# A ReGLU MLP with Strassen-Winograd products: w2 in two column halves, its sums accumulated earlier, the casts of later x moved, and GpSimd's loads held behind the first x rows

## The chip, the cores and the metric

The kernel runs on one core of a Trainium2 chip. The metric is the device time of one execution in microseconds; the times given are the median of three runs. A profile is one further execution taken by the hardware profiler; its span goes from the first to the last instruction.

## The reference

```python
def reference(x, w1, w2):              # x [16, 256, 512], w1 [512, 4096], w2 [2048, 512], all float32
    h = x @ w1
    gate, value = np.split(h, 2, axis=-1)
    h = np.maximum(gate, 0) * value
    return (h @ w2).astype(np.float32)
```

That is 4096 rows of x; a first product to 4096 hidden columns (2048 gates, 2048 values), a product of the two, and a second product back to 512 columns.

## The kernel before

All of it is in `fast_way` (`general_way` runs only if a flag computed from the data says that the numbers don't fit float16; here it doesn't). The 4096 rows are four sets (`NS`) of 1024, each in two halves of 512 (`TH`). Weights and x are float16 on the chip.

**First product.** The 2048 gate columns and as many value columns make 16 blocks (`NJ`) of 128 + 128. A block computes a 2 x 2 product (halves of the 512 inner rows, gate and value, halves of the set) with seven products instead of eight: `P1` to `P7`, each two matmuls of 512 columns. For that it needs sums of x (`S1` to `S4`, `x_sum`, on VectorE) and sums of w1 (`T1` to `T4`, `w1_ops`, L157): for blocks 4 to 15 GpSimd makes them in set 0, for blocks 0 to 3 VectorE does, later. Blocks 0 to 3 of set 0 are therefore computed plainly (`Plain`, L236), with eight products. `PERIOD` and `SLOT` (L25) interleave the seven products of neighbouring blocks.

**Second product.** `mm2_stream` (L271) multiplies the float16 result g by w2 in the same way: seven products P1 to P7 over 8 x 128 rows, for four groups of 128 rows of x, with sums `S1` to `S4` of g (`g_sum`, L264) and sums `T1` to `T4` of w2 (tiles `v_t`). The sums of g are made by GpSimd (S3, and most of S1) and by VectorE (the rest) in set 0. The stream is a Python generator of single matmuls: a set's first 20 are put between its last blocks, its last 8 between the first blocks of the next set, and the rest between the two (`advance`, L337).

**Loads.** x rows of set 0's first half come in float32 by SP (`xf`, in the tile of g's S1; L389), and are turned by TensorE (`turn_pair`, L361: transposes into PSUM, then copies). The first two blocks of w1 come in float32 by ACT (`wl`) and are cast by ACT and VectorE (`cast_w`). Everything else is cast to float16 by DMAs that GpSimd issues: the second half of set 0's x and, later, sets 1 to 3 into DRAM tiles `x16` (`cast_x`, L349), from where SP's transposing DMAs bring them in turned (`turn_by_dma`, L369) and plain row loads bring them for the data check (`fetch_rows`, L379, read by `look_x`); w1 in five more chunks (`fetch_w1`, L342); w2 in four parts of 512 KB, each 4 x 128 full rows (`fetch_w2`, L346). `w2_sb` holds w2 as [128, 16, 512], so the quarters B11, B12, B21, B22 (`V`, L148) have rows of 256 columns = 512 bytes within rows of 1024 bytes.

**The sums of w2** are made by DMA: SP copies a quarter into a `v_t` tile, and GpSimd issues a DMA that adds another quarter to it (`accum_op=ADD`): T1 = B11 + B12, T3 = B12 + B22, T2 = T1 + B22, T4 = T2 + B21 (L506 to L513, L522).

**What sets the order.** The schedule is manual: each engine runs its instructions, the issues of its DMAs among them, in the order in which the program text emits them; semaphores for data are put in by the framework. The order on GpSimd in set 0 is: the identity; the cast of x's second half; ten loads of w1; w1 sums of blocks 4, 5; two loads of w2; sums of blocks 6, 7; two loads of w2; sums of blocks 8, 9; three casts of x; sums of blocks 10, 11; the additions for T1 and T3; sums of blocks 12 to 15; the addition for T2; two S3 sums of g; the addition for T4; two S3 sums; three S1 sums. In sets 1 to 3 it has only sums of g.

Of the kernel before, what the change touches and what calls it, by code (L numbers as in the profile page):

```python
# [9 lines left out]
F32, F32R, F16 = dt.float32, dt.float32r, dt.float16  # L10
# [6 lines left out]
P = 128  # L17
TH = 512
# [81 lines left out]
def fast_way(ctx, tc, x2, w1, w2, out2, flag):  # L100
# [27 lines left out]
    place = {jb + i: (c, i) for c, (jb, n) in enumerate(CHUNKS) for i in range(n)}  # L128
    wr = [wpool.tile([P, 4, 2, n * P], F16, name=f"wr{c}") for c, (_, n) in enumerate(CHUNKS)]
    wt = [wpool.tile([P, 4, 2, n * P], F16, name=f"wt{c}") for c, (_, n) in enumerate(CHUNKS)]  # L130
    w2_sb = wpool.tile([P, NJ, DO], F16, name="w2_sb")
    v_t = {n: wpool.tile([P, NHC, HALF], F16, name=f"v_{n}") for n in ("T1", "T2", "T3", "T4")}
    x16 = {s: dpool.tile([SET, D], F16, name=f"x16_{s}") for s in range(NS)}

    NX = 2 * 2 * NB * NS
    NW = NX + 2 * NP
# [2 lines left out]
    def W(name, jb, n=1):  # L139
        c, i = place[jb]  # L140
        raw = {"B11": (0, 0), "B21": (2, 0), "B12": (0, 1), "B22": (2, 1)}
        js = slice(i * P, (i + n) * P)
        if name in raw:
            e, g = raw[name]
            return wr[c][:, e:e + 2, g, js]
        return wt[c][:, int(name[1]) - 1, :, js]

    V = {"B11": w2_sb[:, :NHC, :HALF], "B12": w2_sb[:, :NHC, HALF:], "B21": w2_sb[:, NHC:, :HALF], "B22": w2_sb[:, NHC:, HALF:],  # L148
         **{n: t for n, t in v_t.items()}}

    TURNS = (("T1", "B12", "B11", ADD), ("T2", "B22", "T1", ADD), ("T3", "B22", "B12", ADD), ("T4", "B21", "T2", ADD))

    def turned(op):
        for t in TURNS:
            op(*t)

    def w1_ops(eng, jb, n):  # L157
        turned(lambda m, a, b, o: eng.tensor_tensor(W(m, jb, n), W(a, jb, n), W(b, jb, n), op=o))  # L158

    warm = tmp.tile([P, 2, TH], F32, name="warm", tag="tmp")  # L160
    warm_b = warm.rearrange("p a t -> p (a t)").bitcast(F16)
    nc.vector.memset(warm[:, 0], 0.0)
    ident = wpool.tile([P, P], F32, name="ident")

    def idle(n):
        for _ in range(n):
# [14 lines left out]
    def look(t, at, of):  # L181
        sq = tmp.tile([P, 1024], F16, name="sq", tag="sq", bufs=1)
        sq = sq[:, :of] if len(t.shape) == 2 else sq[:, :of].rearrange("p (a b) -> p a b", a=t.shape[1])
        nc.scalar.activation(sq, t, SQUARE, scale=(P / of) ** 0.5, accum_out=st[:, at:at + 1])  # L184
# [159 lines left out]
        nc.gpsimd.dma_start(out=wr[c][:, :, g], in_=w1_v[:, :, g, jb * P:(jb + n) * P])  # L344

    def fetch_w2(i):  # L346
        nc.gpsimd.dma_start(out=w2_sb[:, 4 * i:4 * i + 4, :], in_=w2_v[:, 4 * i:4 * i + 4, :])  # L347

    def cast_x(s):  # L349
        nc.gpsimd.dma_start(out=x16[s], in_=x2[s * SET:(s + 1) * SET, :])  # L350
# [5 lines left out]

    g, go = g_tiles()
    xf = go["S1"].rearrange("p a t -> p (a t)").bitcast(F32).rearrange("p (b d) -> p b d", b=NB)
    wl = g[:, NJ - 4:].rearrange("p a t -> p (a t)").bitcast(F32).rearrange("p (e g j) -> p e g j", e=4, g=2)

    def turn_pair(o, b0):  # L361
        for b in (b0, b0 + 1):
            ps = psw.tile([P, 4, P], F32, name="W", tag="W")
            for e in range(4):
                nc.tensor.transpose(ps[:, e], xf[:, b, e * P:(e + 1) * P], ident)
            copy = nc.scalar.copy if b % 2 else nc.vector.tensor_copy
            copy(out=o["A1"][:, :, b * P:(b + 1) * P], in_=ps)

    def turn_by_dma(s, o, h):  # L369
        for k in range(2):  # L370
            nc.sync.dma_start_transpose(out=o[f"A{h + 1}{k + 1}"], in_=x16[s][h * TH:(h + 1) * TH, k * 256:k * 256 + 256])
# [7 lines left out]
    def fetch_rows(s, q):  # L379
        rows[s, q] = xpool.tile([P, 2, D], F16, name=f"xn{q % 2}")  # L380
        nc.sync.dma_start(out=rows[s, q], in_=x16[s][q * 256:(q + 1) * 256].rearrange("(b p) d -> p b d", p=P))

    def look_x(s, i):
        b = i // 2
        t = rows[s, b // 2][:, b % 2] if (s, b // 2) in rows else xf[:, b]
        look(t[:, i % 2 * 256:i % 2 * 256 + 256], 4 * NB * s + i, 256)

    for b in (0, 2):
        nc.sync.dma_start(out=xf[:, b:b + 2], in_=x_v[0, :, b:b + 2])  # L389
    for g_ in range(2):  # L390
        nc.scalar.dma_start(out=wl[:, :, g_], in_=w1_v[:, :, g_, :2 * P])
    make_identity(nc, ident)
    nc.gpsimd.dma_start(out=x16[0][TH:], in_=x2[TH:SET, :])
    for c in range(1, len(CHUNKS)):
        for g_ in range(2):
            fetch_w1(c, g_)

    xo = x_tiles()
    turn_by_dma(0, xo, 1)
    for q in (2, 3):  # L400
        fetch_rows(0, q)
    plain = [Plain(g, jb) for jb in range(NPLAIN)]
    idle(NWARM)
    cast_w(0)
# [15 lines left out]
    for p in plain[2:]:  # L420
        p.open_x()
        p.open_w()
        p.mm(0, xo["A1"], 0, 2)
        p.mm(1, xo["A1"], 0, 2)
        p.close(0)
    sums = list(SUMS)

    def x_sum(o):
# [3 lines left out]
    for p in plain:  # L432
        p.open_x()
        p.open_w()
        p.mm(0, xo["A2"], 0, 2)
        p.mm(1, xo["A2"], 0, 2)
        x_sum(xo)
        if p is not plain[-1]:
            p.close(1)
        look_x(0, p.jb)  # L440
# [3 lines left out]
        look(wr[c][:, :, i % 2, o * P:(o + 2) * P], NX + i, 1024)  # L444

    def look_w2(i):
        look(w2_sb[:, 2 * i:2 * i + 2].rearrange("p h n -> p (h n)"), NW + i, 1024)

    def judge():
        n = st.shape[1]  # L450
# [26 lines left out]
            BESIDE[s, 7 + 2 * i] = [f]  # L477
    BESIDE[NS - 1, 6] = [judge]
    verdict = []
    BESIDE[NS - 1, 20] = [lambda: tc.mark_branch_hint_location("general")]  # L480
    BESIDE[NS - 1, 18] = [lambda: verdict.append(nc.values_load(
        flag[0:1, 0:1], min_val=0, max_val=1, skip_runtime_bounds_check_because="a comparison wrote it"))]

# [3 lines left out]
    for s in range(NS):  # L487
        if s:
            g, go = g_tiles()
        first = NPLAIN if s == 0 else 0  # L490
        blocks = {jb: Block(xo, g, jb) for jb in range(first, NJ)}
        plan = {jb * PERIOD + at: (jb, n) for jb in blocks for n, at in SLOT.items()}
        last = NJ * PERIOD
        stream = mm2_stream(s, go)
        if s == 0:
            w1_ops(nc.gpsimd, 4, 2)
            fetch_w2(0)
            fetch_w2(1)
            w1_ops(nc.gpsimd, 6, 2)
            fetch_w2(2)  # L500
            fetch_w2(3)
            w1_ops(nc.gpsimd, 8, 2)
            for c in range(1, NS):
                cast_x(c)
            w1_ops(nc.gpsimd, 10, 2)
            nc.sync.dma_start(out=V["T1"], in_=V["B11"])  # L506
            nc.sync.dma_start(out=V["T3"], in_=V["B12"])
            nc.gpsimd.dma_start(out=V["T1"], in_=V["B12"], accum_op=ADD)  # L508
            nc.gpsimd.dma_start(out=V["T3"], in_=V["B22"], accum_op=ADD)  # L509
            nc.sync.dma_start(out=V["T2"], in_=V["T1"])  # L510
            w1_ops(nc.gpsimd, 12, 4)
            nc.gpsimd.dma_start(out=V["T2"], in_=V["B22"], accum_op=ADD)
            nc.sync.dma_start(out=V["T4"], in_=V["T2"])  # L513
        for at in range(first * PERIOD, last + PERIOD):
            if at in plan:
                jb, n = plan[at]
                if n == "P1" and s and jb in (4, 8):
                    fetch_rows(s, 1 + jb // 4)
                if n == "P1" and s == 0 and jb in (11, 12, 13, 14):
                    g_sum(nc.gpsimd, go, "S3", 2 * jb - 22, 2 * jb - 20)  # L520
                    if jb == 12:
                        nc.gpsimd.dma_start(out=V["T4"], in_=V["B21"], accum_op=ADD)  # L522
                getattr(blocks[jb], n)()
                if n == "P5":
                    for f in LOOKS.get((s, jb), ()):
                        f()
                if n == "P4" and s:
                    if jb < NHC:
                        g_sum(nc.gpsimd, go, "S3", jb, jb + 1)
                    elif jb < NJ - BY_DVE:  # L530
                        for m in ("S1", "S2", "S4"):
                            g_sum(nc.gpsimd, go, m, jb - NHC, jb - NHC + 1)
            elif at >= last:
                advance(stream, 4)
            else:
                advance(prev, 4)
        if s == 0:
            for h in (0, 2, 4):
                g_sum(nc.gpsimd, go, "S1", h, h + 2)
            g_sum(nc.vector, go, "S1", 6, 8)  # L540
            for m in ("S2", "S4"):
                for h in (0, NHC // 2):
                    g_sum(nc.vector, go, m, h, h + NHC // 2)
        else:
            for m in ("S1", "S2", "S4"):
                g_sum(nc.vector, go, m, NHC - BY_DVE, NHC)
        done = 20
        if s + 1 < NS:
            xo = x_tiles()
            for h in range(2):  # L550
                turn_by_dma(s + 1, xo, h)
            for q in range(2):
                fetch_rows(s + 1, q)
            advance(stream, 100)
            sums = list(SUMS)
            for _ in SUMS:
                x_sum(xo)
            if s == 0:
                w1_ops(nc.vector, 0, 2)
                w1_ops(nc.vector, 2, 2)  # L560
            advance(stream, MM2 - TAIL - 100 - done)
        else:
            advance(stream, MM2)
        prev = stream
# [29 lines left out]
```

## Time and profile before

| what | us |
|---|---|
| median of three runs (lowest, highest) | 345.38 (344.56, 346.49) |
| the profiled execution, its own time | 344.94 |
| its span | 343.2 |
| TensorE (PE) busy | 308.5, 90% of the span |
| VectorE (DVE), ScalarE (ACT), GpSimd (POOL) busy | 217.8, 188.1, 152.6 |
| mean granted TensorE clock | 0.960 |

The profile names an instruction by its line, engine, operation and tiles (written <- read). A number in brackets behind it is the time that its engine was idle before it, and what released it. Matmuls are pipelined, so that the shown length of the last of a group overlaps with the next group; starts are the better measure. SPq or POOLq is the issue of a DMA by SP or GpSimd; its landing is told apart from it. Where a window is named, times count from the span's start. Three of the page's rows by 40 equal slices of the span (8.6 us each; tenths of busy time, or of the full TensorE clock) show where the engines rest:

```
PE   6589993099469999999999999999999999999993
POOL 7289900685940013469900043399500144699000
PEclk9789999579969999999999999999999999999999
```

### The profile page before, as it was taken

The page shows a single profiled execution, that of the slowest core. Times are in us where ns is not written, and L with a number is a line of the kernel's source. Part 1 is how long each engine was busy: PE and PEld are TensorE (multiplying, and loading weights), DVE is VectorE, ACT ScalarE, POOL GpSimd, SP SyncE. Part 2 cuts the span into 40 slices and gives each one's busy share as a digit, 9 for nine tenths or more (in the row PEclk, how much of TensorE's full clock was granted, in tenths as well). Part 3 has the DMA queues.
Part 4 walks back from the last instruction along what each step waited for, and adds up shares of the span by engine and source line. Part 5 has one row for each costly group of instructions (what it writes and reads, how often), then busy time and mean ns, then how long its engine had stood idle before and what let it go on. Part 6 is the DMA issues. An engine that isn't in the chain of part 4 may idle for free.

```text
span 343.2 us, 5085 instructions
## 1 busy us (share of the span) xinstructions
PE 308.5 (90%) x1843; PEld 182.0 (53%) x1843; DVE 217.8 (63%) x328; ACT 188.1 (55%) x449; POOL 152.6 (44%) x133
## 2 busy tenths in 40 slices
PE   6589993099469999999999999999999999999993
PEld 3344441035348744444688544444887444446883
DVE  1147884048997278888843488888551788888401
ACT  2137673045138576667477576666585766764230
POOL 7289900685940013469900043399500144699000
PEclk9789999579969999999999999999999999999999
DMA  7999999788943200100551300100732001000113
GB/s 225 219 204 215 206 240 209 125 135 147 152 71 122 94 31 32 32 0 0 89 158 70 116 32 0 31 2 21 162 128 94 31 31 32 0 1 2 61 63 129
DMA packets 39069, 31.83 MB, mean 93 GB/s; under 512 B 16016, under 2 KB 34192, under 8 KB 38928
## 3 DMA queue, kind: packets, MB, share of 16 engines
q0 software_dynamic: 11728, 11.54, 21.4%
q1 hardware_dynamic: 26112, 18.75, 19.9%
q10 hardware_dynamic: 1200, 1.18, 1.1%
q8 instruction: 16, 0.26, 0.3%
q14 instruction: 13, 0.11, 0.1%
HBM read 24.64 MB, written 12.06 MB: 107 GB/s over the span
## 4 chain that ended last, share of the span: by engine, by line
PE 75%; DMA 15%; POOL 7%; issue 1%; DVE 0%; ACT 0%; POOLq 0%; SPq 0%
PE Y L196 20%; PE W L196 13%; PE X L196 13%; PE Y L278 12%; PE W L278 9%; PE X L278 7%; DMA v_T<-w_sb 6%; DMA w_sb<-in_w_dram 5%; DMA wr<-in_w_dram 4%; POOL g_S L267 3%; POOL wt L158 2%; POOL wr L344 1%; POOL v_T L509 1%; POOL v_T L508 0%; POOL w_sb L347 0%
## 5 line engine op out<-in xcount | busy, mean ns | idle before, releaser
L267 POOL TENSOR_TENSOR g_S<-g 128x512 f16<-128x512 f16 (+1 forms) x49 | 64.4, 1382 | 126.8 <-DVE g L233 124.8
L196 PEld LDWEIGHTS <-wt 128*128 128x128 f16 x480 | 47.0, 98 | 71.3 <-POOL wt L158 14.7
L196 PE MATMUL Y<-x_S,wt 128*128 128x512 f16 x240 | 72.3, 383 | 0.0
L196 PE MATMUL X<-x_A,wr 128*128 128x512 f16 x240 | 71.8, 381 | 0.2 <-ACT Y L203 0.2
L223 DVE SCALAR_TENSOR_TENSOR cc<-W,pu 128x512 f32<-128x512 f32 x60 | 41.5, 692 | 36.9 <-ACT pu L217 35.0
L278 PEld LDWEIGHTS <-g_S 128*128 128x128 f16 x512 | 50.2, 99 | 15.8 <-POOL g_S L267 8.9
L196 PEld LDWEIGHTS <-wr 128*128 128x128 f16 x360 | 35.3, 98 | 42.0 <-issue 2.1
L203 ACT COPY Y<-X 128x512 f32<-128x512 f32 x60 | 34.2, 570 | 39.3 <-PE X L196 20.5
L229 DVE SCALAR_TENSOR_TENSOR cc<-Y,pu 128x512 f32<-128x512 f32 x60 | 40.9, 682 | 14.5 <-PE Y L196 14.4
L196 PE MATMUL W<-x_S,wt 128*128 128x512 f16 x120 | 36.1, 383 | 13.8 <-POOL wt L158 13.8
L217 ACT ACTIVATE pu<-Y 128x512 f32<-128x512 f32 x60 | 35.9, 598 | 15.3 <-PE Y L196 15.3
L210 ACT ACTIVATE pu<-W 128x512 f32<-128x512 f32 x60 | 36.1, 602 | 14.5 <-PE W L196 14.3
L224 DVE SCALAR_TENSOR_TENSOR g<-X,cc 128x512 f16<-128x512 f32 x60 | 41.5, 692 | 2.3
L233 DVE SCALAR_TENSOR_TENSOR g<-Y,cc 128x512 f16<-128x512 f32 x60 | 40.9, 681 | 2.7 <-PE Y L196 2.7
L278 PEld LDWEIGHTS <-g 128*128 128x128 f16 x384 | 37.6, 98 | 8.2
L196 PE MATMUL W<-x_S,wr 128*128 128x512 f16 x120 | 36.2, 383 | 0.0
L196 PE MATMUL Y<-x_A,wt 128*128 128x512 f16 x120 | 35.9, 380 | 0.0
L278 PE MATMUL X<-w_sb,g 128*128 128x256 f16 x256 | 31.2, 272 | 0.0
L278 PE MATMUL Y<-v_T,g_S 128*128 128x256 f16 x256 | 30.7, 273 | 0.0
L308 DVE SCALAR_TENSOR_TENSOR o<-W,pv 128x256 f32<-128x256 f32 x16 | 6.8, 425 | 33.9 <-PE W L278 33.4
L278 PE MATMUL W<-v_T,g_S 128*128 128x256 f16 x128 | 17.9, 288 | 7.8 <-POOL g_S L267 7.8
L184 ACT ACTIVATE sq<-xn 128x256 f16<-128x256 f16 x56 | 23.2, 415 | 0.0
(64 smaller groups left out, 303.3 us busy)
## 6 DMA issues: line engine op xcount, KB each, us to landing
out_dram<-o SPq DMA_DIRECT2D x16, 256.0 KB, 2.1
out_dram<-pv SPq DMA_DIRECT2D x15, 256.0 KB, 2.0
xn<-x SPq DMA_DIRECT2D x14, 256.0 KB, 3.2
x<-in_x_dram POOLq DMA_DIRECT2D x3, 1024.0 KB, 18.7
wr<-in_w_dram POOLq DMA_DIRECT2D x4, 512.0 KB, 20.3
w_sb<-in_w_dram POOLq DMA_DIRECT2D x4, 512.0 KB, 14.8
v_T<-w_sb POOLq DMA_DIRECT2D x4, 512.0 KB, 8.3
wr<-in_w_dram POOLq DMA_DIRECT2D x6, 256.0 KB, 13.4
```

Of the source, the lines that this page charges most:

```text
L158: turned(lambda m, a, b, o: eng.tensor_tensor(W(m, jb, n), W(a, jb, n), W(b, jb, n), op=o))
L184: nc.scalar.activation(sq, t, SQUARE, scale=(P / of) ** 0.5, accum_out=st[:, at:at + 1])
L196: nc.tensor.matmul(ps, W(wn, self.jb)[:, b], self.xo[xn][:, b, :], start=fresh and b == 0, stop=b == 1, skip_group_check=True)
L203: nc.scalar.copy(out=self.Y, in_=self.X)
L210: nc.scalar.activation(self.p5, self.W, COPY, scale=GS)
L217: nc.scalar.activation(self.u2, self.Y, COPY, scale=-GS)
L223: nc.vector.scalar_tensor_tensor(out=self.c12, in0=self.W, scalar=GS, in1=self.u2, op0=MULT, op1=ADD)
L224: nc.vector.scalar_tensor_tensor(out=self.g[:, self.jb, :TH], in0=self.X, scalar=0.0, in1=self.c12, op0=MAX, op1=MULT)
L229: nc.vector.scalar_tensor_tensor(out=self.c22, in0=self.Y, scalar=-GS, in1=self.p5, op0=MULT, op1=ADD)
L233: nc.vector.scalar_tensor_tensor(out=self.g[:, self.jb, TH:], in0=self.Y, scalar=0.0, in1=self.c22, op0=MAX, op1=MULT)
L267: eng.tensor_tensor(go[n][:, h0:h1], go[i0][:, h0:h1], go[i1][:, h0:h1], op=op)
L278: nc.tensor.matmul(ps, go[gn][:, k, b * P:(b + 1) * P], V[vn][:, k, :], start=fresh and k == 0, stop=k == NHC - 1, skip_group_check=True)
```

## The change

- w2 lies in two tiles `w2_h`, one for each half of its columns, as [128, 16, 256], so that a quarter is one stretch of 4 KB in each partition. It is loaded as four quarters of 512 KB (8 x 128 rows of 256 columns).
- SP copies B11, B12, B22, B21 into T1, T3, T2, T4, one after the other; no copy waits for an addition any more. GpSimd's additions are T1 += B12, T3 += B22, T2 += T1, T4 += T2. The first two are issued after two of the four w1 sums of blocks 12 to 15, the third after all four, the last in block 12 as before.
- Set 0's second half of x doesn't go through DRAM: GpSimd's DMA casts it into `xh` (the tile of g's S2), and TensorE turns it with a float16 identity (`turn_half`). `turn_by_dma` and `fetch_rows` of set 0 go.
- GpSimd's first load waits until the first x rows have landed (a copy of one column into `gate`), and x's second half comes after w1's chunk 1 instead of ahead of it.
- The casts of sets 1 to 3 move: set 1's behind the fourth S3 sum in set 0, those of sets 2 and 3 to the first products of blocks 0 and 1 of set 1.
- The hint for the branch at the end names five engines.

```diff
-    w2_sb = wpool.tile([P, NJ, DO], F16, name="w2_sb")
+    w2_h = [wpool.tile([P, NJ, HALF], F16, name=f"w2_{i}") for i in range(2)]
...
-    x16 = {s: dpool.tile([SET, D], F16, name=f"x16_{s}") for s in range(NS)}
+    x16 = {s: dpool.tile([SET, D], F16, name=f"x16_{s}") for s in range(1, NS)}
...
+    V = {f"B{k + 1}{n + 1}": w2_h[n][:, k * NHC:(k + 1) * NHC] for k in range(2) for n in range(2)}
+    V.update(v_t)
...
+    def w1_ops(eng, jb, n):
         for t in TURNS:
-            op(*t)
-
-    def w1_ops(eng, jb, n):
-        turned(lambda m, a, b, o: eng.tensor_tensor(W(m, jb, n), W(a, jb, n), W(b, jb, n), op=o))
+            w1_one(eng, jb, n, *t)
+
+    def w1_one(eng, jb, n, m, a, b, o):
+        eng.tensor_tensor(W(m, jb, n), W(a, jb, n), W(b, jb, n), op=o)
+
+    def add_w2(m, v):
+        nc.gpsimd.dma_start(out=V[m], in_=V[v], accum_op=ADD)
...
-    ident = wpool.tile([P, P], F32, name="ident")
+    ident = {t: wpool.tile([P, P], t, name=f"ident{k}") for k, t in enumerate((F32, F16))}
+    gate = wpool.tile([P, 1], F32, name="gate")
...
     def fetch_w2(i):
-        nc.gpsimd.dma_start(out=w2_sb[:, 4 * i:4 * i + 4, :], in_=w2_v[:, 4 * i:4 * i + 4, :])
+        ks, n = slice(i // 2 * NHC, i // 2 * NHC + NHC), i % 2
+        nc.gpsimd.dma_start(out=w2_h[n][:, ks], in_=w2_v[:, ks, n * HALF:(n + 1) * HALF])
...
+    xh = go["S2"][:, :NB]
...
+    def turn_half(o, b0, copy):
+        ps = psx.tile([P, 4, 2, P], F16, name="X", tag="X")
+        for b in range(2):
+            for e in range(4):
+                nc.tensor.transpose(ps[:, e, b], xh[:, b0 + b, e * P:(e + 1) * P], ident[F16])
+        copy(out=o["A2"][:, :, b0 * P:(b0 + 2) * P], in_=ps.rearrange("p e b t -> p e (b t)"))
...
-        t = rows[s, b // 2][:, b % 2] if (s, b // 2) in rows else xf[:, b]
+        t = rows[s, b // 2][:, b % 2] if s else (xf, xh)[b // NB][:, b % NB]
...
-    make_identity(nc, ident)
-    nc.gpsimd.dma_start(out=x16[0][TH:], in_=x2[TH:SET, :])
-    for c in range(1, len(CHUNKS)):
+    for t in ident.values():
+        make_identity(nc, t)
+    nc.gpsimd.tensor_copy(out=gate, in_=xf[:, 0, :1])
+    fetch_w1(1, 0)
+    fetch_w1(1, 1)
+    for b in (0, 2):
+        nc.gpsimd.dma_start(out=xh[:, b:b + 2], in_=x_v[0, :, NB + b:NB + b + 2])
+    for c in range(2, len(CHUNKS)):
         for g_ in range(2):
             fetch_w1(c, g_)
 
     xo = x_tiles()
-    turn_by_dma(0, xo, 1)
-    for q in (2, 3):
-        fetch_rows(0, q)
...
         p.close(0)
+        if p is plain[2]:
+            turn_half(xo, 0, nc.vector.tensor_copy)
+    turn_half(xo, 2, nc.scalar.copy)
...
-        p.mm(0, xo["A2"], 0, 2)
-        p.mm(1, xo["A2"], 0, 2)
+        if p is plain[0]:
+            for q in range(2):
+                p.mm(0, xo["A2"], q)
+                p.mm(1, xo["A2"], q)
+        else:
+            p.mm(0, xo["A2"], 0, 2)
+            p.mm(1, xo["A2"], 0, 2)
...
-        look(w2_sb[:, 2 * i:2 * i + 2].rearrange("p h n -> p (h n)"), NW + i, 1024)
+        look(w2_h[i % 2][:, i // 2 * 4:i // 2 * 4 + 4].rearrange("p h n -> p (h n)"), NW + i, 1024)
...
-    BESIDE[NS - 1, 20] = [lambda: tc.mark_branch_hint_location("general")]
+    BESIDE[NS - 1, 20] = [lambda: tc.mark_branch_hint_location(
+        "general", engines=[ENG.PE, ENG.SP, ENG.Activation, ENG.DVE, ENG.Pool])]
...
             w1_ops(nc.gpsimd, 8, 2)
-            for c in range(1, NS):
-                cast_x(c)
             w1_ops(nc.gpsimd, 10, 2)
-            nc.sync.dma_start(out=V["T1"], in_=V["B11"])
-            nc.sync.dma_start(out=V["T3"], in_=V["B12"])
-            nc.gpsimd.dma_start(out=V["T1"], in_=V["B12"], accum_op=ADD)
-            nc.gpsimd.dma_start(out=V["T3"], in_=V["B22"], accum_op=ADD)
-            nc.sync.dma_start(out=V["T2"], in_=V["T1"])
-            w1_ops(nc.gpsimd, 12, 4)
-            nc.gpsimd.dma_start(out=V["T2"], in_=V["B22"], accum_op=ADD)
-            nc.sync.dma_start(out=V["T4"], in_=V["T2"])
+            for m, v in (("T1", "B11"), ("T3", "B12"), ("T2", "B22"), ("T4", "B21")):
+                nc.sync.dma_start(out=V[m], in_=V[v])
+            for t in TURNS:
+                w1_one(nc.gpsimd, 12, 4, *t)
+                if t[0] == "T2":
+                    add_w2("T1", "B12")
+                    add_w2("T3", "B22")
+            add_w2("T2", "T1")
         for at in range(first * PERIOD, last + PERIOD):
             if at in plan:
                 jb, n = plan[at]
+                if n == "P1" and s == 1 and jb < 2:
+                    cast_x(2 + jb)
...
                     if jb == 12:
-                        nc.gpsimd.dma_start(out=V["T4"], in_=V["B21"], accum_op=ADD)
+                        add_w2("T4", "T2")
+                    if jb == 14:
+                        cast_x(1)
```

More of the change, by code (lines that the diff above doesn't have):

```diff
@@ L146, in W @@
         return wt[c][:, int(name[1]) - 1, :, js]
-    V = {"B11": w2_sb[:, :NHC, :HALF], "B12": w2_sb[:, :NHC, HALF:], "B21": w2_sb[:, NHC:, :HALF], "B22": w2_sb[:, NHC:, HALF:],
-         **{n: t for n, t in v_t.items()}}
+    V = {f"B{k + 1}{n + 1}": w2_h[n][:, k * NHC:(k + 1) * NHC] for k in range(2) for n in range(2)}
+    V.update(v_t)
     TURNS = (("T1", "B12", "B11", ADD), ("T2", "B22", "T1", ADD), ("T3", "B22", "B12", ADD), ("T4", "B21", "T2", ADD))
-    def turned(op):
+    def w1_ops(eng, jb, n):
         for t in TURNS:
-            op(*t)
-    def w1_ops(eng, jb, n):
-        turned(lambda m, a, b, o: eng.tensor_tensor(W(m, jb, n), W(a, jb, n), W(b, jb, n), op=o))
+            w1_one(eng, jb, n, *t)
[3 more added lines that the diff above has]
+        nc.gpsimd.dma_start(out=V[m], in_=V[v], accum_op=ADD)
     warm = tmp.tile([P, 2, TH], F32, name="warm", tag="tmp")
@@ L364, in turn_pair @@
             for e in range(4):
-                nc.tensor.transpose(ps[:, e], xf[:, b, e * P:(e + 1) * P], ident)
+                nc.tensor.transpose(ps[:, e], xf[:, b, e * P:(e + 1) * P], ident[F32])
             copy = nc.scalar.copy if b % 2 else nc.vector.tensor_copy
             copy(out=o["A1"][:, :, b * P:(b + 1) * P], in_=ps)
+    def turn_half(o, b0, copy):
[4 more added lines that the diff above has]
+        copy(out=o["A2"][:, :, b0 * P:(b0 + 2) * P], in_=ps.rearrange("p e b t -> p e (b t)"))
     def turn_by_dma(s, o, h):
```

## The prediction

> **What bounds the kernel now.** I read the chain that ended last first, in order of time (start, us, piece):
>
> ```profile
> 4.46 14.13 DMA wr<-in_w_dram
> ...
> 24.07 16.59 DMA w_sb<-in_w_dram
> 40.73 21.87 DMA v_T<-w_sb
> ...
> 68.68 1.03 PE W L196 x2
> ...
> 86.80 11.04 POOL g_S L267 x5
> 97.89 2.87 PE W L278 x12
> ...
> 169.28 3.06 PE X L278 x28
> ...
> 188.06 2.62 PE Y L278 x24
> ```
>
> From 68.68 on it is TensorE nearly alone; before that it is loads, w2's copies and GpSimd. So two holes in TensorE's work are to be looked for in set 0; its own timeline has them in brackets (idle before, releaser):
>
> ```profile
> 13.89 1.87 PE L251 MATMUL W<-x_A,wr 128*128 128x256 f16 x8 [1.87 <-DVE x_A L367]
> ...
> 30.41 0.59 PE L196 MATMUL X<-x_A,wr 128*128 128x512 f16 x2
> ...
> 54.28 0.59 PE L196 MATMUL X<-x_A,wr 128*128 128x512 f16 x2
> 68.68 1.03 PE L196 MATMUL W<-x_S,wt 128*128 128x512 f16 x2 [13.80 <-POOL wt L158]
> ...
> 73.68 0.59 PE L196 MATMUL X<-x_A,wr 128*128 128x512 f16 x2
> ...
> 85.84 3.22 PE L278 MATMUL X<-w_sb,g 128*128 128x256 f16 x28
> 93.75 0.39 PE L278 MATMUL W<-v_T,g_S 128*128 128x256 f16 x2 [4.69 <-POOL g_S L267]
> ...
> 117.41 0.59 PE L196 MATMUL X<-x_A,wr 128*128 128x512 f16 x2
> ```
>
> Hole one, at block 12: a matmul of 256 columns takes 0.109 us (2.62 for 24 in the chain), so a pair of 512 columns 0.44. From 54.7 (54.28 and one pair) to 73.68 is 19.0 us for six pairs, which need 2.6. It costs **16.4 us**: 13.8 idle and some 2.6 in slow pairs after it (the first takes 1.03 in the chain). Hole two, at the second product: 85.84 to 117.41 is 31.6 us; the same work in set 1 goes from 169.28 to 190.68, 21.4 us. It costs **10.2 us**. From 117.41 on, 225.8 us follow without holes. Both holes end at GpSimd (POOL), so its timeline comes next:
>
> ```profile
> 18.74 1.16 POOL L158 TENSOR_TENSOR wt<-wr 128x512 f16<-128x512 f16 x1 [3.34 <-DMA wr<-in_w_dram]
> ...
> 63.23 1.65 POOL L508 DMA_DIRECT2D v_T<-w_sb  x1 [20.43 <-DMA v_T<-w_sb]
> ...
> 85.85 1.56 POOL L522 DMA_DIRECT2D v_T<-w_sb  x1 [4.28 <-DMA v_T<-v_T]
> ```
>
> At L508 POOL stands 20.4 us for a copy of a quarter of w2; behind it in its queue are the w1 sums of blocks 12 to 15, and so comes hole one. At L522 it stands 4.3 us; behind it are two S3 sums and the three S1 sums of g (the 11.04 us of the chain, ending at 97.84), and so comes hole two.
>
> **The change, part by part.** *Block 12.* T1 and T2 of blocks 12 to 15 now stand ahead of any wait for w2's copies, only T3 and T4 behind two additions. Hole one's 16.4 us go if those copies land by about 53. Their landing times (KB each, median us):
>
> ```profile
> v_T<-w_sb POOLq DMA_DIRECT2D x4, 512.0 KB, 8.3
> ...
> v_T<-w_sb SPq DMA_DIRECT2D x2, 512.0 KB, 22.3
> v_T<-v_T SPq DMA_DIRECT2D x2, 512.0 KB, 4.2
> x<-in_x_dram POOLq DMA_DIRECT2D x3, 1024.0 KB, 18.7
> ...
> x_A<-x SPq DMA_TRANSPOSE x14, 4.1
> ```
>
> The 22.3 were 512-byte pieces beside three casts of x; 4.2 is a copy of long rows (v_T to v_T) beside little. Now rows are long and the casts gone, while the second half of w2 still loads: bounds 4.2 and 22.3, I take 7. With w2's first half in at about 41 (40.73 above) T1's copy lands near 48, POOL arrives there at about 48, and T3 and T4 are done near 55, when block 12 first needs them.
>
> The Trainium skill, DMA: Bandwidth & Descriptors, section Why small descriptors are slow (HBM only), says that copies from SBUF to SBUF don't pay for short descriptors. By it only the missing traffic helps, and the additions would land no sooner for their longer rows; the two rows above differ in both things and can't decide it. This is the rival of slow additions below.
>
> *POOL becomes the bound of set 0.* With its waits gone, what is left is its own work, from these groups (busy, mean ns):
>
> ```profile
> L267 POOL TENSOR_TENSOR g_S<-g 128x1024 f16<-128x1024 f16 x7 | 15.9, 2740 | 0.0
> ...
> L158 POOL TENSOR_TENSOR wt<-wr 128x512 f16<-128x512 f16 x8 | 9.9, 1238 | 3.4 <-DMA wr<-in_w_dram 3.3
> L158 POOL TENSOR_TENSOR wt<-wr,wt 128x512 f16<-128x512 f16 x8 | 9.6, 1205 | 0.3
> ...
> L158 POOL TENSOR_TENSOR wt<-wr 128x1024 f16<-128x1024 f16 x2 | 5.1, 2538 | 0.0
> ...
> L158 POOL TENSOR_TENSOR wt<-wr,wt 128x1024 f16<-128x1024 f16 x2 | 4.2, 2115 | 0.1
> ...
> L347 POOL DMA_DIRECT2D w_sb<-in_w_dram x4 | 3.0, 766 | 0.0
> ...
> L350 POOL DMA_DIRECT2D x<-in_x_dram x3 | 1.6, 523 | 0.0
> ```
>
> Its first sum waits for chunk 2 of w1 (18.74). The gate stands ahead of all of GpSimd's loads until the first x rows (5.35, below); they were issued from about 2 on: by the issue it would land 3.3 later, 22; by the bytes, which are the same except for set 0's transposes and row loads that vanish, 17. I take 18. Then: 16 sums 19.5; four loads of w2, now 1024 rows each where 512 took 0.77 and 1024 (L508) 1.65, so 1.55 each, 6.2 (bounds 3.0 and 6.6); the larger sums 9.3; four additions of 128 long rows each, not seen here, between 0.5 (L350, the cheapest issue) and 1.65, I take the lower, being nearer in rows, 2.1; four S3 and three S1 sums 15.9; one cast's issue 0.5; gaps 1. That is 54.5, and S1 could end at 72.5.
>
> The chain of additions is the other limit. Two additions of before by themselves, the one issued between 75 and 76 us and the one after 84 (KB, us to landing):
>
> ```profile
> v_T<-w_sb POOLq DMA_DIRECT2D x1, 512.0 KB, 6.4
> ```
> ```profile
> v_T<-w_sb POOLq DMA_DIRECT2D x1, 512.0 KB, 10.8
> ```
>
> In the changed order T1 is issued near 48, T2 waits until it has landed, T4 until T2 has; behind T4 stand two S3 sums, the cast and S1, 4.6 + 0.5 + 6.7. So S1 ends no earlier than 48.5 + 1 + 11.8 + 2A = 61.3 + 2A, A being one landing. With 6.4 it is 74.1, with 8.3 77.9, with 4.2 (a copy's time) the work decides. I take 73.5. Before it was 97.84, and from there to the end everything followed it (VectorE's S1 part and S2, S4 come after): **24.3 us less**, a span of 318.9. TensorE's own limit is lower: 343.2 less 16.4, 10.2 and the start's gain, 2.7 (below), is 313.9; it would want S1 by 69.9 (85.84 + 3.2 - 16.4 - 2.7). So some 3.5 us of hole two stay.
>
> *Start.* The held loads leave the first ones alone:
>
> ```profile
> 5.35 1.06 PE L365 MATMUL W<-ident,g_S 128*128 128x128 f32 x8 [0.29 <-DMA g_S<-in_x_dram]
> ```
> ```profile
> 12.81 0.62 ACT L374 CAST wr<-g 128x512 f16<-128x512 f32 x1 [5.25 <-DMA g<-in_w_dram]
> ```
>
> Two of the four first loads (512 KB each) were there by 5.35 to 6.4, some 4.3 after their issue; the other two, alone, need as long again, so the second half of the first w1 rows lands at about 9.7, not 12.81, and the W product starts some 3 us sooner than 13.89 (0 to 4). The second half of x is now turned by TensorE: 16 f16 transposes at most 2.1 us (8 f32 took 1.06), and two copies out of PSUM beside them, against the 0.9 us that TensorE waited for the DMA's transposes; net gain 2.7. The transposes wait for rows whose load is third and fourth behind the gate; block 3's first half is queued behind them, and those rows should be there by 16, it by 18. The gain is worth nothing while POOL is the bound. If the clock, cold from 12 to 19, also stayed up, 2.6 more (an estimate: as much as the slow pairs after hole one). The second identity and the gate's copy (under 1 us of POOL) lie ahead of the first x rows and cost nothing.
>
> *The casts of x.* Set 1's is issued after S3, 7 us ahead of S1's end. Those of sets 2 and 3 stand in the code at set 1's first blocks, but POOL has nothing to wait for there: it issues them right behind S1. So they run while set 1's transposes do. Three casts of 1 MB needed 18.7 in the median beside w2's rest; alone I take 7 (5 to 18.7), so x of set 1 lands at S1's end, T. Then the transposes; alone and beside loads:
>
> ```profile
> 82.88 6.60 SPq L371 DMA_TRANSPOSE x_A<-x  x4
> ```
> ```profile
> x_A<-x SPq DMA_TRANSPOSE x2, 10.8
> ```
>
> The second line is the median of the two issued between 9 and 20 us, beside w1's casts. So the last of four lands between T+10 (5 of issue and 4.1 to 4.4) and T+20 (twice that, as 10.8 is over twice 4.1); I take T+15. Behind them on VectorE are:
>
> ```profile
> 106.60 0.68 DVE L430 TENSOR_TENSOR x_S<-x_A 128x1024 f16<-128x1024 f16 x1
> ...
> 114.18 0.42 DVE L308 SCALAR_TENSOR_TENSOR o<-W,pv 128x256 f32<-128x256 f32 x1 [1.92 <-PE W L278]
> ```
>
> The x sums began at T+8.8 with 1.9 to spare before L308, so T+11 (0.3 more in what follows L308) is free and T+15 costs **4 us**: L308 and L313 stand behind, TensorE's last product of set 0 waits for L313. Bounds 0 and 9.
>
> By the Trainium skill, DMA: Bandwidth & Descriptors, section Queues, rings and completion order, the engines take turns between queues by packets. Then the transposes would keep half of the engines and lose little, which is a part of rival 1; the 10.8 above against 4.1 alone speaks against it.
>
> *Without weight in the sum.* SP loses set 0's transposes, the row loads and the two copies that waited for additions, and gets four copies behind w2; it is idle there. The looks read x from other tiles with the same shapes. The casts of sets 2 and 3 are wanted 70 us later. The branch hint on named engines may shorten this one on TensorE:
>
> ```profile
> L45 PEldq COMPARE_BRANCH x1: 3806/3806/3806, 336.7 to 336.7; - x1
> ```
>
> It ends 2.7 before the span does (336.7 + 3.8 against 343.2), while the last output lands and the engines meet; between nothing and 2.7, I take nothing, as other engines are still waiting then.
>
> **Sum.** 343.2 - 24.3 + 4 = 322.9 of span; the profiled execution took 344.94, 1.74 beyond its span; 324.6. The median of the runs, 345.38, is 0.4 above the profiled one, which I leave in the range.
>
> **Rivals.**
> 1. *TensorE stays the bound*: POOL issues w2 at the old 0.77 and additions land in 4 (S1 by 70), transposes lose nothing. 313.9 + 1.7 = 315.6; 313 if the clock stays up at the start. For it: from 60 on nothing but the additions and one cast is left to load. Against: POOL's work alone sums to 72.5.
> 2. *Slow additions and starved transposes*: A of 8.3 to 10.8 gives T of 78 to 83, and the transposes cost 8: 343.2 - 17.4 + 8 + 1.7 = 335.5; with one of the two, 329 to 330.
> 3. *The change doesn't take away hole one*: the copies land in 22.3 as before. Then T1's addition is issued at 63, T2's at 71, T4's at 78, S1 ends at 90 with A near 7, and with 9 for the transposes it is 343.2 - 7.8 + 9 + 1.7 = 346, no change. For it: the same 512 KB and part of the load. Against: the 4.2 row.
> 4. *Slower*: the additions themselves. By 61.3 + 2A and 4 for the transposes it is slower from A = 17.3 on (T at 96); at 20 it is 343.2 + 3.5 + 4 + 1.7 = 352. Nothing but the copies' 22.3 shows such a time, and that was beside 3 MB of casts.
>
> **Chances.** Forecast 0.45 (319 to 329, its own terms one at a time), TensorE bound 0.20, rival 2 0.25, no change 0.04, slower 0.06. Range 314 to 335: it reaches into rivals 1 and 2. About 0.5% is what a measurement here can tell from no change: faster 0.90, same 0.04, slower 0.06.
>
> **What would show it.** After: no idle time over 2 us in TensorE before L196 of block 12; POOL busy almost without holes from 18 to 73; one hole of 2 to 5 us in TensorE before the first W of the second product, released by POOL g_S; the casts of sets 2 and 3 issued within 2 us of S1's end; the first x_S of set 1 waiting for the transposes; 73.1 us for sets 1 and 2 as before. Wrong if POOL waits over 5 us in all at its additions, if chunk 2 lands after 21, or if set 1's transposes land beside the casts as fast as alone.

## The result, and the profile after

| | before | changed |
|---|---|---|
| median of four runs (lowest, highest), us | 344.97 (344.49, 346.49) | 325.22 (324.59, 325.75) |
| span of the profiled execution | 343.2 | 323.5 |
| TensorE busy | 308.5, 90% | 305.7, 95% |

The ratio of the changed kernel to the one before is 0.942, 95% interval 0.9384 to 0.9455. The forecast was 324.6.

TensorE's timeline of the changed kernel (start, us; a bracket is idle time before it and what ended it) shows both holes again:

```profile
25.88 0.59 PE L200 MATMUL X<-x_A,wr 128*128 128x512 f16 x2
...
49.74 0.59 PE L200 MATMUL X<-x_A,wr 128*128 128x512 f16 x2
50.17 0.59 PE L200 MATMUL W<-x_S,wt 128*128 128x512 f16 x2
...
65.26 3.22 PE L282 MATMUL X<-w,g 128*128 128x256 f16 x28
...
70.45 0.39 PE L282 MATMUL W<-v_T,g_S 128*128 128x256 f16 x2 [1.53 <-POOL g_S L271]
71.01 1.26 PE L282 MATMUL W<-v_T,g_S 128*128 128x256 f16 x10 [0.17 <-DVE g_S L271]
...
95.12 1.86 PE L282 MATMUL Y<-v_T,g 128*128 128x256 f16 x8 [5.86 <-DVE pv L317]
96.78 1.06 PE L200 MATMUL X<-x_A,wr 128*128 128x512 f16 x2
```

Blocks start at 25.88 instead of 30.41 (4.5 us gained). The second and third lines are block 12's first products: the W that waited 13.8 us for GpSimd has no bracket. From the first block to the X of the second product (65.26, 85.84 before) it is 39.4 us instead of 55.4: hole one is gone, 16.0 us. But from there to set 1's first block (96.78) it is 31.5 us, as long as before (31.6): **hole two has not become smaller, it has changed its owner.** The wait for S1 is small now; the larger one, 5.9 us, is for L317, VectorE's last step on the output of the second product. After 96.78 follow 226.7 us, 0.9 more than before. So -4.5 - 16.0 - 0.1 + 0.9 = -19.7 us of span.

GpSimd's timeline of the changed kernel shows where S1 stands, and what follows it:

```profile
6.39 0.18 POOL L407 COPY gate<-g_S 128x1 f32<-128x1 f32 x1 [4.49 <-DMA g_S<-in_x_dram]
...
19.39 1.15 POOL L158 TENSOR_TENSOR wt<-wr 128x512 f16<-128x512 f16 x1 [1.78 <-DMA wr<-in_w_dram]
...
46.53 1.86 POOL L161 DMA_DIRECT2D v_T<-w  x2
...
52.74 0.86 POOL L161 DMA_DIRECT2D v_T<-v_T  x1
...
58.54 0.86 POOL L161 DMA_DIRECT2D v_T<-v_T  x1 [0.70 <-DMA v_T<-v_T]
...
63.30 0.81 POOL L355 DMA_DIRECT2D x<-in_x_dram  x1
63.87 6.52 POOL L271 TENSOR_TENSOR g_S<-g 128x1024 f16<-128x1024 f16 x3
70.09 1.25 POOL L355 DMA_DIRECT2D x<-in_x_dram  x2
```

From 19.39 to 70.39 its only wait is 0.70 us. The last line is the casts of sets 2 and 3, issued before S1's last sum was quite over. SP's transposes of set 1, the landing of two of them (window 74 to 76 us), and VectorE's first x sum:

```profile
72.96 13.27 SPq L384 DMA_TRANSPOSE x_A<-x  x4
```
```profile
x_A<-x SPq DMA_TRANSPOSE x2, 11.7
```
```profile
88.39 0.69 DVE L448 TENSOR_TENSOR x_S<-x_A 128x1024 f16<-128x1024 f16 x1 [9.15 <-DMA x_A<-x]
```

Four transposes took 13.3 us to issue instead of 6.6, and VectorE stood 9.2 us for them. L312 and L317 stood behind it. The DMA queues show what the transposes did meanwhile (packets, MB, share of 16 engines; q0 carries GpSimd's DMAs, here the casts, q1 SP's), from 73 to 81.5 us and from 81.5 to 86.3:

```profile
q0 software_dynamic: 64, 1.57, 88.2%
q1 hardware_dynamic: 30, 0.01, 0.6%
```
```profile
q1 hardware_dynamic: 2608, 0.65, 103.1%
...
q0 software_dynamic: 16, 0.00, 0.2%
```

So the transposes did not run slowly beside the casts: they moved next to nothing until the casts were through.

### The profile page after: what moved, and what is told of

Its sections match the earlier page's. It is cut to its first block, busy times and chain, and to the rows that moved or that the text cites. A ratio compares the mean times of both kernels' runs of the same rounds, so it can differ in the third digit from the quotient of the medians.

```text
span 323.5 us, 5143 instructions
## 1 busy us (share of the span) xinstructions
PE 305.7 (95%) x1867; PEld 183.0 (57%) x1867; DVE 211.5 (65%) x329; ACT 189.2 (58%) x450; POOL 151.5 (47%) x137
## 3 DMA queue, kind: packets, MB, share of 16 engines
q0 software_dynamic: 10704, 11.54, 21.9%
## 4 chain that ended last, share of the span: by engine, by line
PE 69%; DVE 0%; ACT 0%; issue 0%
PE Y L200 19%; PE X L200 13%; PE W L200 13%; PE Y L282 11%; PE W L282 6%; PE X L282 6%; ACT pv L323 0%; DVE pv L317 0%; DVE o L312 0%; PE W L485 0%
## 5 line engine op out<-in xcount | busy, mean ns | idle before, releaser
L200 PE MATMUL Y<-x_S,wt 128*128 128x512 f16 x240 | 71.4, 379 | 0.0
L200 PEld LDWEIGHTS <-wr 128*128 128x128 f16 x360 | 35.1, 98 | 41.3 <-issue 0.5
L207 ACT COPY Y<-X 128x512 f32<-128x512 f32 x60 | 34.2, 570 | 39.4 <-PE X L200 21.4
L237 DVE SCALAR_TENSOR_TENSOR g<-Y,cc 128x512 f16<-128x512 f32 x60 | 40.9, 682 | 2.8 <-PE Y L200 2.8
L233 DVE SCALAR_TENSOR_TENSOR cc<-Y,pu 128x512 f32<-128x512 f32 x60 | 40.9, 681 | 0.1
L282 PE MATMUL X<-w,g 128*128 128x256 f16 x256 | 31.2, 272 | 0.0
L312 DVE SCALAR_TENSOR_TENSOR o<-W,pv 128x256 f32<-128x256 f32 x16 | 6.7, 424 | 31.6 <-PE W L282 31.6
L323 ACT ACTIVATE pv<-Y 128x256 f32<-128x256 f32 x16 | 6.1, 382 | 32.0 <-PE Y L282 32.0
L282 PE MATMUL Y<-v_T,g 128*128 128x256 f16 x128 | 17.1, 281 | 5.9 <-DVE pv L317 5.9
## 6 DMA issues: line engine op xcount, KB each, us to landing
w<-in_w_dram POOLq DMA_DIRECT2D x4, 512.0 KB, 10.9
```

The costliest lines, as they stand in the source:

```text
L200: nc.tensor.matmul(ps, W(wn, self.jb)[:, b], self.xo[xn][:, b, :], start=fresh and b == 0, stop=b == 1, skip_group_check=True)
L207: nc.scalar.copy(out=self.Y, in_=self.X)
L233: nc.vector.scalar_tensor_tensor(out=self.c22, in0=self.Y, scalar=-GS, in1=self.p5, op0=MULT, op1=ADD)
L237: nc.vector.scalar_tensor_tensor(out=self.g[:, self.jb, TH:], in0=self.Y, scalar=0.0, in1=self.c22, op0=MAX, op1=MULT)
L282: nc.tensor.matmul(ps, go[gn][:, k, b * P:(b + 1) * P], V[vn][:, k, :], start=fresh and k == 0, stop=k == NHC - 1, skip_group_check=True)
L312: nc.vector.scalar_tensor_tensor(out=d["o1"][:, HALF:], in0=d["W"], scalar=1 / GS, in1=d["pu"][:, 1], op0=MULT, op1=ADD)
```

## The experiments

Times are medians, ratios are to the kernel before, with 95% intervals.

| run | us | ratio (interval) |
|---|---|---|
| changed kernel | 325.22 | 0.942 (0.9384, 0.9455) |
| E1 casts of sets 2, 3 later | 317.32 | 0.9193 (0.9168, 0.9217) |
| E2 E1, cast of set 1 earlier | 324.76 | 0.9412 (0.9384, 0.944) |
| E3 short rows | 329.63 | 0.9552 (0.9524, 0.958) |
| E4 casts where they were | 332.39 | 0.9617 (0.9591, 0.9643) |
| E5 old start | 329.53 | 0.9542 (0.9509, 0.9575) |
| E6 E2, old start | 326.65 | 0.9475 (0.9441, 0.9509) |
| E7 no gate | 324.67 | 0.9397 (0.9371, 0.9422) |
| E8 E2, no gate | 323.22 | 0.9371 (0.9345, 0.9397) |
| E9 E1, no gate | 316.76 | 0.9159 (0.9142, 0.9176) |
| E10 E1, S1 split | 315.94 | 0.9147 (0.9128, 0.9166) |
| E11 E1, S1 split, no gate | 314.73 | 0.9107 (0.9092, 0.9121) |
| E12 E1, old start | 319.68 | 0.9248 (0.9234, 0.9262) |

**E1: what holds up set 1's transposes.** The two casts move behind sums of set 1, which wait for its blocks:

```diff
-                if n == "P1" and s == 1 and jb < 2:
-                    cast_x(2 + jb)
...
                         g_sum(nc.gpsimd, go, "S3", jb, jb + 1)
+                        if s == 1 and jb < 2:
+                            cast_x(2 + jb)
```

> The casts of sets 2 and 3 are issued behind GpSimd's first two sums of set 1, not right behind S1. If they are what held up set 1's transposes (13.3 us of issue, 11 to 12 to landing in the changed kernel), the four issue in about 7 us from x's landing at 73, the last lands near 84 instead of 88.4, TensorE's 5.9 us wait for L317 shrinks to 1 to 2.5, and the time is 320 to 321.5 (325.2 for the changed kernel). Rival: it is the late landing of set 1's own cast (9.5 us after 63.3) that counts; then the transposes still end after 87 and the time stays within 1 us of 325.

It was 317.32, better than expected. SP's timeline, VectorE's and TensorE's in E1:

```profile
72.44 5.38 SPq L384 DMA_TRANSPOSE x_A<-x  x4
```
```profile
80.53 0.69 DVE L448 TENSOR_TENSOR x_S<-x_A 128x1024 f16<-128x1024 f16 x1 [1.69 <-DMA x_A<-x]
```
```profile
70.05 0.39 PE L282 MATMUL W<-v_T,g_S 128*128 128x256 f16 x2 [1.67 <-POOL g_S L271]
...
89.57 0.59 PE L200 MATMUL X<-x_A,wr 128*128 128x512 f16 x2
```

x landed as late as in the changed kernel, but the transposes issue in 5.4 us, VectorE waits 1.7 us instead of 9.2, and set 1 starts 19.6 us after S1's end (70.0), as it did before the change (97.84 to 117.41). In the changed kernel it was 26.4. So the two casts cost 6.8 us there, and some 0.9 behind it, nearly all in slow pairs after the idle time (96.78 is the first of them; the granted clock from 95 to 100 us was 0.67). The rival, set 1's own late cast, falls.

**E2: set 1's cast earlier.** On top of E1, `cast_x(1)` stands ahead of `add_w2("T2", "T1")`.

> As the run before, and set 1's cast is issued ahead of the addition for T2 (near 52) instead of behind the fourth S3 sum (63). If both places of the casts hold up the transposes, they now start when TensorE frees x's tiles, about 63, land by 73, VectorE never waits for them, set 1 starts 20 us after S1's end (70.4), and the time is 318 to 319.5. Rival: the cast, now beside the addition for T2, slows the chain of additions; POOL then waits 3 to 5 us at T4's and S1 ends that much later: 321 to 323.

The rival came, and stronger: 7.4 us slower than E1. GpSimd's and TensorE's timelines:

```profile
65.84 0.87 POOL L161 DMA_DIRECT2D v_T<-v_T  x1 [8.01 <-DMA v_T<-v_T]
66.46 10.67 POOL L271 TENSOR_TENSOR g_S<-g 128x1024 f16<-128x1024 f16 x5
```
```profile
73.05 0.61 PE L282 MATMUL W<-v_T,g_S 128*128 128x256 f16 x2 [5.55 <-POOL g_S L271]
```

T2's addition, issued 1 us after a cast of 1 MB on the same queue, made POOL wait 8.0 us instead of 0.7, and S1 ended at 77.1. Set 1 began 19.6 us after that (96.74), as in E1, so the earlier cast gained nothing there. The chain of additions has no room for a transfer ahead of it.

**E3 and E4: rows or traffic.** E3 keeps w2 in one tile, so that its quarters have rows of 512 bytes; E4 keeps the long rows and puts the three casts where they were:

```diff
+    w2_sb = wpool.tile([P, NJ, DO], F16, name="w2_sb")
-    w2_h = [wpool.tile([P, NJ, HALF], F16, name=f"w2_{i}") for i in range(2)]
+    w2_h = [w2_sb[:, :, i * HALF:(i + 1) * HALF] for i in range(2)]
```

(E3's data check of w2 reads the same elements in another order.)

> w2 lies in one tile as before, so that the copies and additions read rows of 512 bytes; all else is as in the changed kernel. If the missing casts are what made the copies fast (rows don't matter inside SBUF), copies land in 4 to 7 us, additions in 5 to 7, and the time is 325 to 326. If the rows matter, the copies take over 10 us, the additions' issue goes back to 1.6 us each (3 us more of POOL) and POOL waits at T1's or T4's addition: S1 ends 3 to 8 us later and the time is 328 to 333.

> The three casts of x are issued where they were before, ahead of the sums of blocks 10 and 11; rows of w2 stay long. If the casts beside them made the copies slow, T1's copy takes 15 to 22 us again, POOL waits 5 to 15 us at T1's addition, TensorE has a hole of 3 to 12 us at block 12, and the time is 324 to 332, although set 1's transposes are no longer held up. If the long rows made the copies fast, they land in under 8 us, there is no hole at block 12, and with x of set 1 early the time is 319 to 321.

The DMA issues (KB each, median us to landing; SP's copies, then GpSimd's first two additions) in the changed kernel, in E3 and in E4:

```profile
v_T<-w SPq DMA_DIRECT2D x4, 512.0 KB, 4.9
...
v_T<-w POOLq DMA_DIRECT2D x2, 512.0 KB, 7.1
v_T<-v_T POOLq DMA_DIRECT2D x2, 512.0 KB, 5.0
```
```profile
v_T<-w_sb SPq DMA_DIRECT2D x4, 512.0 KB, 7.3
...
v_T<-w_sb POOLq DMA_DIRECT2D x2, 512.0 KB, 10.1
```
```profile
v_T<-w SPq DMA_DIRECT2D x4, 512.0 KB, 11.3
...
v_T<-w POOLq DMA_DIRECT2D x2, 512.0 KB, 19.0
```

Short rows cost half as much again (7.3 against 4.9, 10.1 against 7.1). In time they cost 4.4 us, as E3's second theory had it, although its copies stayed under 10 us; most of it is POOL's chain, in which S1 ends 3.2 us later (73.55).

With the casts in their old place copies and additions took more than twice as long (11.3, 19.0), but the median of the copies mixes two kinds. E4's copies for T1 (window 35 to 35.1), T3 (37 to 40) and T2 (45.2 to 46):

```profile
v_T<-w SPq DMA_DIRECT2D x1, 512.0 KB, 6.2
```
```profile
v_T<-w SPq DMA_DIRECT2D x1, 512.0 KB, 6.4
```
```profile
v_T<-w SPq DMA_DIRECT2D x1, 512.0 KB, 16.1
```

The first two went as fast as in the changed kernel (6.1, 6.5). So GpSimd's wait is not at T1's addition, as I expected, but at T2's:

```profile
65.49 0.87 POOL L161 DMA_DIRECT2D v_T<-v_T  x1 [12.09 <-DMA v_T<-w]
```
```profile
80.96 0.61 PE L282 MATMUL W<-v_T,g_S 128*128 128x256 f16 x2 [13.33 <-POOL g_S L271]
```

T1 and T3 could be issued near 47 even so, behind them stand only two sums, and block 12 has no hole. So hole one goes in E4 too. That long rows alone would do it isn't shown: in E4 w2's first quarter had landed by 35.08, and T1's copy went out 1.8 us ahead of the casts (36.88); in the kernel before it went out at 40.73, 4.1 us behind them, and took 21.9. What the casts' new place takes away is waiting in hole two, 12.1 us at T2's addition and 2.5 at T4's. The 7.2 us that it is worth are a net: in the profiled executions S1 ends 14.7 us later in E4 (85.05), and set 1 begins 20.8 us after it instead of 26.4.

**E5 and E12: the start of before** (no gate, x's second half through DRAM and turned by DMA, chunk 1 behind it) in the changed kernel and in E1.

> The start of before in the changed kernel: no gate, x's second half cast into DRAM first and turned by DMA. Blocks then start about 4.5 us later (30.4, not 25.9). Theory: POOL and then set 1's casts and transposes are the bound, so this costs nothing: S1 ends within 1 us of 70.4, time 324 to 326. Rival: TensorE's start is on the path, and the time grows by 2.5 to 4.5 us, to 328 to 330.

> The kernel with late casts (317.3 us) with the start of before: blocks start about 5 us later (31.0 to 31.5, not 25), and set 0's transposes and row loads are on the DMA queues again beside w1 and w2. With TensorE nearly the bound the start counts: TensorE is done with X of the second product near 72.5, S1 ends near 72.8, and the time is 320 to 322. Rival: w2's loads land later as well (15.5 us, as in the changed kernel with the old start), POOL waits longer at the additions, and the time is 323 or more.

E5 refutes me: 4.3 us slower. GpSimd's timeline and w2's loads in E5:

```profile
49.53 0.88 POOL L161 DMA_DIRECT2D v_T<-w  x1 [1.79 <-DMA w<-in_w_dram]
```
```profile
w<-in_w_dram POOLq DMA_DIRECT2D x4, 512.0 KB, 15.5
```

Chunk 2 came at the same time (19.40), but w2 landed later (15.5 us after issue, 10.9 with the new start), POOL waited for it, and S1 ended at 72.8, 2.4 us later. The transposes again stood behind the casts (15.0 us of issue), and set 1 began at 101.1, another 1.9 us later. E5 changes the start and the load on the DMA queues together and doesn't part them. In E12, where no casts interfere, S1 ended at 72.8 too, as I expected, and the old start costs 0.0055 of the time before, some 2 us, a little less than I expected (320 to 322).

**E7 and E9: the gate alone.** `gate` and its copy are left out.

> The changed kernel without the gate alone (GpSimd's loads are issued from 2 us on, order unchanged). Theory: chunk 2 of w1 lands 1 to 3 us earlier (16.5 to 18.5, 19.4 with the gate), POOL's chain ends as much earlier, S1 at 67.5 to 69.5, set 1's cast too, and the time falls by 1 to 3 us, to 322 to 324, although TensorE's W product starts up to 2 us later (11.6 with the gate). Rival: the gate only moves bytes, chunk 2 lands within 0.7 us of 19.4, and the time stays within 1 us of 325.

> The kernel with the casts of sets 2 and 3 behind GpSimd's first sums of set 1 (317.3 us), without the gate. Theory: the gate only trades TensorE's start (1 to 1.5 us later without it) for POOL's (S1 1 to 2 us earlier), so the time stays within 1 us of 317.3. Rival: the gate is worth the 2.5 us or more by which TensorE's W product began earlier than in the kernel before: 319 to 320.

No run shows a gain from the gate: without it the kernel is some 0.6 us faster in both, with intervals that overlap. E7's theory had the steps right, GpSimd's first sum at 17.39 (19.39 with the gate) and the end of S1 at 69.1 (70.4), but the time fell by less. TensorE's W product comes at 11.94 (11.56 with the gate, 13.89 in the kernel before), the blocks start at 26.25 (25.88). So the gate is worth 0.4 of the 4.5 us by which the blocks start earlier; the rest comes with the new order of loads and TensorE's transposes, which no run parts.

**E6 and E8** put the old start and the missing gate into E2.

> The same start of before in the kernel whose casts of x are out of the way of set 1's transposes. There TensorE is nearly the bound: with blocks starting 4.5 us later it wants S1 at about 72.8, after POOL has it (70). Theory: now the start costs 2 to 3.5 us against that kernel. Rival: POOL stays the bound there too, and the start costs under 1 us.

> The kernel with the casts out of the way, without the gate. Theory: POOL's S1 comes 1 to 3 us earlier, TensorE's hole before the first W of the second product (2.1 us) goes, but blocks start 1 to 2 us later, so that TensorE becomes the bound: within 1.5 us of the kernel with the gate. Rival: TensorE's start counts in full, 2 us slower.

As E2 turned out to be bound by its chain of additions, they don't test what they were made for: 1.9 us slower, and 1.5 us faster without the gate.

**E10 and E11: the rest of hole two.** POOL's third S1 sum goes to VectorE; E11 is without the gate as well.

```diff
-            for h in (0, 2, 4):
+            for h in (0, 2):
                 g_sum(nc.gpsimd, go, "S1", h, h + 2)
-            g_sum(nc.vector, go, "S1", 6, 8)
+            g_sum(nc.vector, go, "S1", 4, 8)
```

> The same kernel (317.3 us) with the third of POOL's S1 sums given to VectorE, which then makes two quarters in one instruction. If POOL's S1 is what is left of hole two, POOL ends near 67.8 instead of 70, S1 is whole near 69.1 instead of 70.6, TensorE's 1.7 us hole shrinks to under 0.7, and the time falls by 0.8 to 1.6 us, to 315.7 to 316.5. Rival: VectorE, which also makes S2 and S4 behind it, becomes the bound and the time stays within 0.4 us of 317.3.

> Both: no gate and the third S1 sum on VectorE. With POOL ahead by then, TensorE alone is the bound, and its later start counts: 316 to 318, not faster than the kernel with the split and the gate. Rival: POOL is still late there, and the time falls under 315.7.

E10 met its theory (315.94). E11's rival came: 314.73, outside E10's interval. TensorE's timeline of E11 at the second product:

```profile
65.69 3.22 PE L281 MATMUL X<-w,g 128*128 128x256 f16 x28
68.75 1.91 PE L281 MATMUL W<-v_T,g_S 128*128 128x256 f16 x16
70.50 1.91 PE L281 MATMUL Y<-v_T,g_S 128*128 128x256 f16 x16
72.24 2.02 PE L281 MATMUL W<-w,g_S 128*128 128x256 f16 x16
...
87.20 0.59 PE L199 MATMUL X<-x_A,wr 128*128 128x512 f16 x2
```

No bracket is left: hole two is closed, 65.69 to 87.20 is 21.5 us, the length that it has in the other sets. E11 is the fastest kernel of the study, 3.2% below the changed one. Without the gate POOL's last S1 sum ended 0.9 us earlier than in E10 (67.09, 68.01), and the time fell by 1.2 us: of four pairs of kernels with and without the gate, all are faster without it, this one clearly.

## Why the prediction was right, step by step

**Hole one** goes in full, but the prediction named two things, and only one is seen at work: copies that land in time. T1's copy went out at 34.77, as the quarter of w2 that it needs landed 6 us sooner than the 41 taken for the first half, and landed 6.1 us later (7 taken), at 40.9; T3's landed at 43.9. POOL came to their additions at 46.53 and found no wait. The other thing, that T1 and T2 of blocks 12 to 15 stand ahead of the wait, is worth little here: with the additions first, from 42.3 on, POOL would have waited about 1 us for T3's copy. That is an estimate from these times; no run puts the additions back.

**POOL as the bound of set 0** is right: no wait over 0.7 us from 19.4 to 70.4, S1 behind it, one small hole in TensorE (1.5 us before the W, where 2 to 5 were forecast). The sum came out 3.1 us too high, 73.5 against 70.4. Two terms missed in opposite ways, as the changed kernel's groups (busy, mean ns of one) show:

```profile
L352 POOL DMA_DIRECT2D w<-in_w_dram x4 | 3.6, 900 | 0.0
...
L161 POOL DMA_DIRECT2D v_T<-w x2 | 1.9, 1082 | 0.0
L161 POOL DMA_DIRECT2D v_T<-v_T x2 | 1.7, 862 | 0.8 <-DMA v_T<-v_T 0.7
```

w2's four issues took 3.6, not 6.2: an issue does not follow the number of rows (twice the rows, 0.90 against 0.77). The additions took 3.6, not 2.1. In E3 the two with short rows took 3.2 together. Chunk 2 came at 19.4, not 18, since the first x rows themselves came later, at 6.4. What my sum counted apart also overlaps: an issue's end and the next sum's start do by 0.6 us at 46.53.

**The chain of additions**: A was 7.1 for the first two, 5.0 for T2; by 61.3 + 2A it would have been 73.4. It began 2 us sooner than I took (46.5), and T2 was issued by POOL's own pace. Rival 2's first half was close, though: E2 shows what a single MB ahead of T2 does.

**The start** was named as 2.7 us and worth nothing. It was 4.5: W began 2.3 us sooner, and the first 24 matmuls from there took 2.6 us instead of 5.1, at a granted clock of 1.00 instead of 0.51 (12 to 19 us). The prediction had named that as "2.6 more" and left it out of its sum. E5 shows that undoing the start costs 4.3. The step that failed is "worth nothing while POOL is the bound": I let the start act by TensorE alone, but with the old start w2 also lands later, POOL's additions wait for w2, and S1 ends 2.4 us later (2.8 in E12). That set 0's transposes and row loads are what held w2 up is an argument; the order of loads changes with them.

**The casts of sets 2 and 3** were the right mechanism with too small a size: 4 us taken, 6.8 and about 0.9 found, so 7.7 of the bounds' 9. x landed 2.6 us after S1's end, not with it (its cast took 9.5 us, not 7), and the last transposes at T+18, not T+15, T being S1's end. E1 shows that the casts do it; the working had the transposes run at half their pace beside them, the queues show them standing until the casts were through.

So 324.6 against 325.2 is partly luck: S1 was 3.1 us earlier than forecast and the transposes cost 3.7 more.

**The rule on short descriptors** from the Trainium skill (DMA: Bandwidth & Descriptors, section Why small descriptors are slow (HBM only)) does not hold here as it stands: with the casts away in both, copies inside SBUF landed in 7.3 with 512-byte rows and in 4.9 with 4 KB. What the prediction drew from it for the missing traffic agrees with E4, where T2's copy took 16.1 us beside the casts.

Half of the engines, which the prediction drew from the turns by packets of the Trainium skill (same page, section Queues, rings and completion order), is not what set 1's transposes got: their queue moved 0.01 MB while the casts' moved 1.57. The turns themselves are not refuted by it, if the profile's packets are the page's: the casts' 64 packets were of some 25 KB each, the 2608 that followed on the transposes' queue of 250 bytes.

**The branch hint**: TensorE's branch fell from 3.8 to 0.4 us; ScalarE's last copy stood 5.2 us ahead of the span's end before (337.99 of 343.2) and 5.4 after (318.12 of 323.5). It gave nothing.

## What to carry to other kernels

In a schedule by hand, an instruction stands in time where its engine's queue lets it stand, not where the text puts it: a DMA placed "in the next set" goes out at once if its engine has nothing to wait for, and it is held back by putting it behind an instruction that really waits. When a wait goes, look at what the freed engine starts next and who needs the same DMA engines then: here over a quarter of the gain (7.9 of 28 us) was lost that way and came back by moving two lines. And where two stages meet, compare the stretch between them with the same stretch in a stage without holes: hole two kept its 31.5 us although its cause was another.

## What the runs showed of the hardware

A VectorE sum of two SBUF operands that meets a run of GpSimd sums waits for the whole run, not for one of them. In the changed kernel's VectorE timeline its S1 part has 4.76 us:

```profile
66.19 4.76 DVE L271 TENSOR_TENSOR g_S<-g 128x1024 f16<-128x1024 f16 x1
```

It ends at 70.95, just behind GpSimd's last S1 sum (70.39); when it came up, one of those sums had just begun and another was still to come. In the kernel before, where it met five sums, it had 11.62 us. In all ten profiles in which this sum meets GpSimd's it ends 0.56 to 0.57 us behind the last of them, in E3 (8.95 us) although the issue of a cast lay between two of the sums. Where it came up while GpSimd stood waiting for a DMA, as in E2 and E4, it took 0.69 us.

That explains why handing VectorE more work made S1 whole sooner. In E10, with one GpSimd sum less, VectorE's sum of twice the size ended at 69.10, 1.1 us behind GpSimd's last; in E1 the smaller one ended at 70.55.
